# A decoder trunk on one core: the order in which two stages' weights are loaded and split

## The chip, the cores and the metric

The kernel runs on one core of a Trainium2 chip. The metric is the device time in microseconds (us) of one execution; the kernel before has a median of 1101.56 us over three runs (1101.03 to 1102.16).

## The reference

One layer of a decoder trunk on 512 positions of width 1024, in float32. Three token mixers work in parallel on a normalised input; their outputs are gated, projected and summed, the sum is projected once more, normalised and added to the input, and a SwiGLU block follows.

```python
gates = jax.nn.sigmoid(mg).reshape(B, S, N_BRANCH, D_MODEL)
merged = (gates[:, :, 0] * (y_a @ w_br_a)
          + gates[:, :, 1] * (y_b @ w_br_b)
          + gates[:, :, 2] * (y_c @ w_br_c))
x = x + rms_norm(merged @ w_o, g_post_mix)

hf = rms_norm(x, g_pre_ffn)
f_gate, f_up = jnp.split(hf @ w_ffn_in, 2, axis=-1)
f = (jax.nn.silu(f_gate) * f_up) @ w_ffn_out
return x + rms_norm(f, g_post_ffn)
```

The change lies between the gate and projection of the second branch (`y_b @ w_br_b`) and the first products with `w_ffn_in`.

## The kernel before, in words

**Split matmuls.** Every matrix is multiplied at float32 accuracy out of fast `fp32r` matmuls: a weight tile of 128x1024 is loaded as it is (`raw`), ScalarE copies it into a rounded `hi` (line 131), VectorE computes the rest `lo = raw - hi` (line 136), and TensorE adds three products, `hi*x_hi`, `hi*x_lo` and `lo*x_hi`. So each weight tile costs one DMA of 512 KB on SyncE's queue, one ScalarE and one VectorE instruction, and it must have passed all three before TensorE comes to it. The `raw` tiles have two buffers: the load of a tile waits for the `lo` of the tile two places earlier in that ring.

**The weight list.** `wlist` holds the tiles in the order of their use. `wload(upto)` issues load and split of all tiles below `upto`, but not beyond `wlimit`; `unit()` hands out the next tile and calls `wload` for two further ones. `tc.issue_after(ins)` keeps what is issued inside it behind the instruction `ins` in the engines' order; without it the layer that orders the program may put it earlier. Each engine then carries out its own list strictly in that order. `B0 + j` are the gate tiles 0 to 7 of branch b, `B0 + 8 + k` (k = 0 to 7) the tiles of `w_o`, and `W0 + i` (`W0 = B0 + 16`; i = 0 to 3) the first gate/up tiles of `w_ffn_in`. The text calls them gate j, w_o k and fi i.

**The stages around the change.**
- `b_stage` computes branch b's gates (`b_gate`, 24 matmuls of 128x512 each) and its projection in four pairs (`b_pair(0)` to `b_pair(3)`, 84 matmuls of 128x256 each). A pair's weights are loaded by `b_raw` into `raw` tiles (pairs 0 and 1) or into another slab (`rawb`), and are turned by `b_prep` into sums and splits (lines 1124 to 1163): `a22`, then the differences of lines 1141, 1142, 1152, 1153, and the splits that give `a11`, `s2`, `a12`, `s1`/`s4`, `s3`. Within a pair, ScalarE empties the one accumulator `z` between products (lines 1186 to 1205), and the next product on `z` waits for that copy. `i` in `b_stage` counts a pair's steps.
- `wo_pass(0)` and `wo_pass(2)` multiply by `w_o` (line 1332): each pass takes two of the four row chunks, goes through the eight tiles of `w_o` in order, and makes 12 matmuls with each. The tiles stay for the second pass. A pass uses four of six accumulator banks, so the second pass takes its third and fourth bank from the first pass, whose results must have been read by then.
- Beside `wo_pass(0)` run `row_loads` (rows of `x`, the gain vectors `gb`, and w_o tiles 4 to 7) and `first_weights`, which loads the first pair of gate/up tiles for the later stage (`rawp`, one DMA of 1 MB) and prepares it in `pair_prep` (lines 1548 to 1562: `s13`, `a22`, the sums of 1557 and 1559, and the splits). Here `s13` takes a `raw` buffer too.
- Beside `wo_pass(2)` run `wo_norm(0)` and `gain_late`. `wo_norm(0)` reads each bank of pass 0 twice: squares on ScalarE (line 1349, `junk`) and products with the gain on VectorE (line 1352, `yg`), which free the bank. `gain_late` scales the second gain vector.
- `ffn_head` multiplies by fi 0 to 3 (line 262), and `pairs` goes on with the rest.

**What sets the order.** The order on each engine comes from the order in which these generators issue, and from `issue_after`. In `b_stage` gate 4 is loaded by `b_more(1)` at step 3 of pair 0 and gate 5 by the `b_more(1)` behind that pair, which keeps it behind the pair's last copy of `z`; w_o 0 to 4 are issued at steps 1, 3, 5, 7 and 9 of pair 3, each behind the last copy of `z`; fi 0 and the next are issued by `unit()` towards the end of pass 0, since `wlimit` is already at its end.

Of the kernel before, what the change touches and what calls it, by code (L numbers as in the profile page):

```python
# [52 lines left out]
def hybrid_block(ctx: ExitStack, tc: tile.TileContext, A, out):  # L53
# [44 lines left out]
    def nm(s):  # L98
        cnt[0] += 1
        return f"{s}_{cnt[0]}"  # L100

    def slab(name, dt=F32, tag="slab", shape=(4, S), first=0):
        pool, bufs = (merge if tag == "m" else big, TAGS[tag]) if tag in TAGS else phase_pool[tag]
        if tag not in ("y", "mo", "f"):
            return pool.tile([128, *shape], dt, tag=tag, name=nm(name), bufs=bufs)
        size = 2064 if tag == "f" else 2112
        t = pool.tile([128, size], dt, tag=tag, name=nm(name), bufs=bufs)[:, first:first + math.prod(shape)]
        return t if len(shape) == 1 else t.rearrange(
            "p (a b) -> p a b" if len(shape) == 2 else "p (a b c) -> p a b c", **dict(zip("abc", shape)))

    def row(name, dt=F32, tag="row", first=0):
        bufs = {"row": 6, "q32": 2, "tg": 2}[tag]
        return mid.tile([128, S if tag == "row" else S + 32], dt, tag=tag, name=nm(name), bufs=bufs)[:, first:first + S]
# [13 lines left out]
    def f32(ap):  # L127
        return ap.bitcast(F32)

    def split(src, hi, lo, lo_eng=None):  # L130
        res["hi"] = SC.activation(hi, src, AF.Copy)  # L131
        e = lo_eng or V
        if e is GP:
            GP.tensor_sub(lo, src, f32(hi))
        else:
            res["lo"] = V.tensor_sub(lo, src, f32(hi))  # L136

    res = {}
# [32 lines left out]
    B0 = len(wlist)  # L171
# [5 lines left out]
    W0 = len(wlist) - 2 * HEAD  # L177
    WALL = len(wlist)
    wlimit = [B0 + 4]
# [13 lines left out]
    def wload(upto):  # L193
        while wnext[0] < min(upto, wlimit[0]):
            i = wnext[0]
            ap, tag = wlist[i]
            if isinstance(ap, tuple):
                hi = wts.tile([128, 1024], F32R, tag="hi", name=nm("hi"), bufs=3)
                lo = wts.tile([128, 1024], F32R, tag="lo", name=nm("lo"), bufs=3)
                fo["prep"](*ap, hi, lo)  # L200
                wready[i] = (hi, lo)
                wnext[0] += 1
                continue
            raw = stage.tile([128, 1024], F32, tag="raw", name=nm("raw"), bufs=2)
            parts = [slice(0, 512), slice(512, 1024)] if i == 0 else [slice(0, 1024)]
            for n, p in enumerate(parts):
                (SC if i == n == 0 else SY).dma_start(raw[:, p], ap[:, p])
                if i == 0:
                    x_in(n + 1)
            if i == W0:  # L210
                u = slab("u", F32R, tag, (2, 1024))
                near = row("uh", F32R, "tg", 32), row("ul", F32R, "q32", 32)
                split(raw[:, :512], *near)
                split(raw[:, 512:], u[:, 0, 512:], u[:, 1, 512:])
                wready[i] = tuple(Halved(near[n], u[:, n]) for n in range(2))
                wnext[0] += 1
                continue
            if tag == "gate":

                hi = lo = wts.tile([128, 1024], F32R, tag="hi", name=nm("hi"), bufs=3)  # L220
                SC.activation(hi, raw, AF.Copy)
                r, h = (t.rearrange("p (k m) -> p k m", m=128)[:, :, 64:] for t in (raw, hi))
                V.tensor_sub(h, r, f32(h))
                wready[i] = (hi, lo)
                wnext[0] += 1
                continue
            if tag:
                u = slab("u", F32R, tag, (2, 1024))
                hi, lo = u[:, 0], u[:, 1]
            else:  # L230
                hi = wts.tile([128, 1024], F32R, tag="hi", name=nm("hi"), bufs=3)
                lo = wts.tile([128, 1024], F32R, tag="lo", name=nm("lo"), bufs=3)
            todo = [(raw[:, p], hi[:, p], lo[:, p], V) for p in parts]
            if i == 0:
                wfirst.extend(todo)
            else:
                split(*todo[0])
            wready[i] = (hi, lo)
            wnext[0] += 1
# [41 lines left out]
    def x_in(k):  # L281
        SY.dma_start(xt[k], A["xT"][:, k, :])
# [830 lines left out]
    def b_raw(p):  # L1113

        if p < 2:
            br[p] = [stage.tile([128, 1024], F32, tag="raw", name=nm("raw"), bufs=2) for _ in range(2)]
        else:
            t = slab("rawb", tag="mo", shape=(2, 1024))
            br[p] = [t[:, i] for i in range(2)]
        for i in range(2):  # L1120
            SY.dma_start(br[p][i], A["w_br"][1, 2 * p + i])
# [3 lines left out]
    def b_prep(p):  # L1125

        r = br.pop(p)
        a11, a12, a21, a22 = (r[i // 2][:, i % 2 * 512:i % 2 * 512 + 512] for i in range(4))
        w = bw[p] = {}

        def pair_unit():
            return tuple(wts.tile([128, 1024], F32R, tag=t, name=nm(t), bufs=3) for t in ("hi", "lo"))

        def halves(u, *names):
            for i, n in enumerate(names):
                w[n] = tuple(t[:, 512 * i:512 * i + 512] for t in u)

        w["a22"] = row("a22h", F32R), row("a22l", F32R)
        split(a22, *w["a22"])
        with tc.issue_after(res["lo"].ins):  # L1140
            V.tensor_sub(a21, a11, a21)
        V.tensor_add(a22, a22, a21)
        yield
        halves(pair_unit(), "a11", "s2")
        split(a11, *w["a11"])
        split(a22, *w["s2"])
        yield
        tag = ("q32", "tg")[p % 2]
        w["a12"] = row("a12h", F32R, tag, 32), row("a12l", F32R, tag, 0)
        split(a12, *w["a12"])  # L1150
        yield
        V.tensor_sub(a11, a22, a11)
        V.tensor_sub(a12, a12, a22)
        yield
        u = pair_unit()
        split(r[0], *u)
        halves(u, "s1", "s4")
        yield
        halves(pair_unit(), "s3")
        split(a21, *w["s3"])  # L1160
        yield

    def b_gate(j):

        ps = bank("mm")
        yield from matrix(ps, hh, hl)
        if j == 2:
            mg["rows"] = slab("tanh", tag="gb")
        t = mg["b", j] = row("tg", tag="tg") if j < 2 else mg["rows"][:, j % 4]
        res["tanh"] = SC.activation(t, ps, AF.Tanh, scale=0.5)  # L1170
# [55 lines left out]
    def b_more(n):  # L1226

        wlimit[0] += n
        with tc.issue_after(res["out"].ins):
            wload(wlimit[0])  # L1230

    def b_stage():

        for p in (0, 2, 3):
            b_raw(p)
        prep = b_prep(0)

        def begin():
            yield from yb_split(2)
            rest = yb_rest()  # L1240
            for g in (prep, prep, rest, rest, prep, prep, prep, rest, rest, prep, rest):
                next(g)
                yield

        run([b_gate(2), b_gate(3)], begin(), 1.5)
        for p in range(4):
            pair = b_pair(p)
            gates = {0: (4, 5), 1: (6,), 2: (7,), 3: ()}[p]
            prep = b_prep(p + 1) if p < 3 else iter(())
            for i, _ in enumerate(pair, 1):  # L1250
                if p < 3:
                    if i == 3:
                        b_more(1)
                    if p and i in (4, 5, 6, 7, 9):
                        next(prep)
                else:
                    if i == 1:
                        wlimit[0] = WALL
                    if i == 2:
                        low_late()  # L1260
                    if i in (1, 3, 5, 7, 9):
                        with tc.issue_after(res["out"].ins):
                            wload(B0 + 9 + (1, 3, 5, 7, 9).index(i))
            if p == 0:
                b_more(1)
                b_raw(1)
                next(prep)
            for n, j in enumerate(gates):
                side = iter(()) if p else itertools.islice(prep, 3 if n == 0 else 1)
                run([b_gate(j)], side, 1.0)  # L1270
            for _ in prep:
                pass
# [36 lines left out]

    def gain_late():  # L1310

        for _ in range(4):
            yield 1
        V.tensor_scalar(res["gb"][:, 1], res["gb"][:, 1], -0.5, None, op0=OP.mult)

    def wo_pass(c0):

# [687 lines left out]
```

## Time and profile before

| | |
|---|---|
| median of three runs | 1101.56 us (1101.03 to 1102.16) |
| the profiled execution | 1103.44 us, of which its span is 1101.7 us |
| TensorE busy | 1090.3 us, 99% of the span |
| VectorE busy | 855.5 us, 78% |
| ScalarE busy | 642.7 us, 58% |
| granted TensorE clock, mean | 0.998 |

In a row of the timeline stand the start and the duration in us, the engine, the line, the operation, the tiles as out<-in, and the count; a bracket tells how long the engine stood idle before it and what it waited for. A DMA-issue row has the engine SPq. Matmuls overlap: a 128x512 matmul shows 0.39 us, though one starts every 0.227 us in a full stream.

### The profile page before, as it was taken

The numbers are of one execution on the slowest core, as the hardware profiler recorded it, in microseconds if no ns is written. First come the engines' busy times: TensorE is split into PE (matmuls) and PEld (weight loads), VectorE is DVE, ScalarE is ACT, GpSimd is POOL, SyncE is SP. The second block draws the span as 40 slices with busy tenths as digits, with TensorE's granted clock in tenths as the row PEclk, the third lists the DMA queues.
The fourth block names the chain that finished last, engine by engine and source line by source line (L and its number), as shares of the span: only waits on it lengthen the run. The fifth ranks groups of instructions, "written<-read, shape, count | busy, mean of one in ns | idle before, by whom it ended". The sixth has DMA issues, their size and how long they took to land.

```text
span 1101.7 us, 16368 instructions
## 1 busy us (share of the span) xinstructions
PE 1090.3 (99%) x6296; PEld 946.7 (86%) x6296; DVE 855.5 (78%) x1500; ACT 642.7 (58%) x1167; POOL 46.3 (4%) x59
## 2 busy tenths in 40 slices
PE   9999999999999999999999999999999999999997
PEld 8888778888888888898888788987999999998886
DVE  6966968263576799998998887867988888889665
ACT  6756674232344676877777655545666565667552
POOL 1000203010000000000000000000000000022200
PEclk9999999999999999999999999999999999999999
DMA  8322325322322210202111134172223233378902
GB/s 314 115 96 77 97 83 189 129 77 97 94 84 90 77 58 20 78 20 77 59 38 59 58 115 134 40 256 69 78 96 120 92 118 114 134 199 224 181 29 95
DMA packets 34941, 115.04 MB, mean 104 GB/s; under 512 B 3440, under 2 KB 3728, under 8 KB 33968
## 3 DMA queue, kind: packets, MB, share of 16 engines
q1 hardware_dynamic: 28064, 96.93, 25.8%
q0 software_dynamic: 5216, 11.18, 5.1%
q10 hardware_dynamic: 1584, 5.90, 1.4%
q8 instruction: 49, 0.80, 0.3%
q14 instruction: 28, 0.23, 0.1%
HBM read 111.89 MB, written 2.10 MB: 103 GB/s over the span
## 4 chain that ended last, share of the span: by engine, by line
PE 91%; DVE 4%; DMA 2%; ACT 2%; issue 1%; DVEq 0%; ACTq 0%
PE mm L262 37%; PE mm L1570 17%; PE mm L1706 7%; PE mm L565 4%; PE o L915 4%; PE sc L877 3%; PE mm L1182 3%; PE tr L902 3%; PE tr L1706 3%; PE mm L793 2%; PE mm L1332 2%; PE tr L709 1%; DMA raw<-in_w_o 1%; DVE lo L136 1%; PE mm L1434 1%; PE tr L490 1%
## 5 line engine op out<-in xcount | busy, mean ns | idle before, releaser
L262 PE MATMUL mm<-hh,hi 128*128 128x512 f32 x504 | 199.6, 396 | 0.0
L262 PE MATMUL mm<-hh,lo 128*128 128x512 f32 x504 | 197.6, 392 | 0.2 <-DVE lo L136 0.2
L262 PE MATMUL mm<-hl,hi 128*128 128x512 f32 x504 | 197.1, 391 | 0.0
L131 ACT ACTIVATE hi<-raw 128x1024 fp32r<-128x1024 f32 (+1 forms) x108 | 110.7, 1026 | 119.1 <-PE mm L262 55.6
L136 DVE TENSOR_TENSOR lo<-raw,hi 128x1024 fp32r<-128x1024 f32 (+1 forms) x108 | 128.3, 1189 | 63.1 <-ACT hi L131 56.8
L262 PEld LDWEIGHTS mm<-hh,lo 128*128 128x128 f32 x504 | 94.7, 188 | 19.9 <-DVE lo L136 0.5
L262 PEld LDWEIGHTS mm<-hh,hi 128*128 128x128 f32 x504 | 94.7, 188 | 18.5 <-ACT hi L131 0.4
L262 PEld LDWEIGHTS mm<-hl,hi 128*128 128x128 f32 x504 | 94.7, 188 | 18.4 <-issue 0.2
L883 ACT ACTIVATE P<-P,ast 128x128 f32<-128x128 f32 (+3 forms) x128 | 70.7, 555 | 23.4 <-DVE ast L881 22.7
L881 DVE CUSTOM_DVE_ANT_0 P<-sc,mask 128x128 f32<-128x128 f32 (+3 forms) x128 | 57.9, 484 | 8.1 <-PE sc L877 7.2
L131 ACT ACTIVATE ph<-tr 128x512 fp32r<-128x512 f32 x80 | 46.9, 592 | 26.0 <-PE tr L902 24.1
L136 DVE TENSOR_TENSOR pl<-tr,ph 128x512 fp32r<-128x512 f32 x80 | 54.4, 685 | 3.0 <-PE o L915 0.9
L1657 POOL DMA_DIRECT2D bs<-in_w_fo x16 | 19.3, 1213 | 781.0 <-DVE lo L136 781.0
L877 PE MATMUL sc<-K,q 128*128 128x512 f32 (+2 forms) x192 | 51.0, 368 | 0.2 <-DVE ast L881 0.2
L1570 PE MATMUL mm<-t,hi 128*128 128x256 f32 x288 | 50.9, 276 | 0.0
L1706 PE MATMUL mm<-hi,u 128*128 128x512 f32 x160 | 50.4, 390 | 0.1
L902 PE MATMUL tr<-ident,P 128*128 128x128 f32 x320 | 48.7, 273 | 0.0
L902 PEld LDWEIGHTS tr<-ident,P 128*128 128x128 f32 x320 | 39.0, 140 | 9.8 <-DVE pl L136 1.1
L136 DVE TENSOR_TENSOR lo<-bs,hi 128x1024 fp32r<-128x1024 f32 x28 | 34.1, 1221 | 13.6 <-ACT hi L131 13.5
L1570 PEld LDWEIGHTS mm<-t,hi 128*128 128x128 f32 x288 | 43.4, 188 | 0.0
L1570 PE MATMUL mm<-fh,hi 128*128 128x256 f32 x144 | 40.1, 278 | 0.0
L1570 PE MATMUL mm<-t,lo 128*128 128x256 f32 x144 | 39.8, 276 | 0.0
(451 smaller groups left out, 2838.1 us busy)
## 6 DMA issues: line engine op xcount, KB each, us to landing
raw<-in_w_in SPq DMA_DIRECT2D x64, 512.0 KB, 3.5
rawp<-in_w_fi SPq DMA_DIRECT2D x20, 1024.0 KB, 4.9
raw<-in_w_br SPq DMA_DIRECT2D x20, 512.0 KB, 3.5
bs<-in_w_fo POOLq DMA_DIRECT2D x20, 512.0 KB, 6.7
w<-in_cw ACTq DMA_DIRECT2D x4, 1024.0 KB, 5.8
raw<-in_w_o SPq DMA_DIRECT2D x8, 512.0 KB, 3.7
bs<-in_w_fo SPq DMA_DIRECT2D x8, 512.0 KB, 7.5
raw<-in_w_v SPq DMA_DIRECT2D x7, 512.0 KB, 5.0
```

Source lines behind the costliest of these rows:

```text
L131: res["hi"] = SC.activation(hi, src, AF.Copy)
L136: res["lo"] = V.tensor_sub(lo, src, f32(hi))
L262: res["mm"] = PE.matmul(ps[:m, n0:n1], w[:, k * 128:k * 128 + m], x[k][:, n0:n1], start=(t == 0), stop=(t == 3 * NK - 1))
L565: res["mm"] = PE.matmul(b[c], x[k][:, c * 128:(c + 1) * 128], w[:, kk * 512:kk * 512 + 512], start=(k == 0 and t == 0), stop=(k == NK - 1 ...
L877: PE.matmul(ps[:, :w * n].rearrange("p (b n) -> p b n", b=w), lhs, K[:, i, brs[0]:brs[-1] + 1, :n], start=(i == 0), stop=(i == 1))
L881: V.tensor_tensor_reduce(out=t, in0=ps[:, b * n:b * n + n], in1=mask[0][:, S - n:], scale=-0.125, scalar=3.0e38, op0=OP.add, op1=OP.min, a ...
L883: SC.activation(t, t, AF.Exp, scale=-1.0, bias=st[:, 0, j, b:b + 1], accum_out=st[:, 1, j, b:b + 1])
L902: PE.transpose(pt[:, j * 128:(j + 1) * 128], self.part(j, br)[:, kt * 128:(kt + 1) * 128], ident)
L915: PE.matmul(po, VV[:, kt, g % 2, br].rearrange("p i d -> p (i d)"), x, start=(br == 0 and kt == 0 and t == 0), stop=(br == 1 and kt == a a ...
L1182: res["mm"] = PE.matmul(ps, u[:, k * 128:k * 128 + 128], v[:, k], start=(start and k == t == 0), stop=(k == 3 and t == 2), skip_group_chec ...
L1570: res["mm"] = PE.matmul(ps, w[:, k * 128:k * 128 + 128], x[:, k], start=(start and k == t == 0), stop=(k == 3 and t == 2), skip_group_chec ...
L1706: PE.matmul(ps, a, b, start=id(ps) not in begun, stop=i == len(ops) - 1, skip_group_check=True)
```

## The change

Three edits.
- Gate 5: where `b_more` raises the limit to `B0 + 6`, its load and split are no longer kept behind the last copy of `z`.
- w_o 0 to 4 are issued at steps 1, 2, 3, 5 and 7 of pair 3 instead of 1, 3, 5, 7 and 9, the first two of them without `issue_after`.
- The limit in pair 3 is `W0` instead of the end, so that `unit()` no longer issues fi 0 in pass 0. `gain_late` raises it at its second step and issues fi 0, then fi 1 and fi 2 each two steps later; fi 3 comes by `unit()`.

```diff
--- before.py
+++ after.py
@@ -1226,7 +1226,7 @@
     def b_more(n):
 
         wlimit[0] += n
-        with tc.issue_after(res["out"].ins):
+        with tc.issue_after(res["out"].ins) if wlimit[0] != B0 + 6 else nullcontext():
             wload(wlimit[0])
 
     def b_stage():
@@ -1255,12 +1255,12 @@
                         next(prep)
                 else:
                     if i == 1:
-                        wlimit[0] = WALL
+                        wlimit[0] = W0
                     if i == 2:
                         low_late()
-                    if i in (1, 3, 5, 7, 9):
-                        with tc.issue_after(res["out"].ins):
-                            wload(B0 + 9 + (1, 3, 5, 7, 9).index(i))
+                    if i in (1, 2, 3, 5, 7):
+                        with tc.issue_after(res["out"].ins) if i > 2 else nullcontext():
+                            wload(B0 + 9 + (1, 2, 3, 5, 7).index(i))
             if p == 0:
                 b_more(1)
                 b_raw(1)
@@ -1309,9 +1309,16 @@
 
     def gain_late():
 
-        for _ in range(4):
+        for n in range(4):
             yield 1
+            if n == 1:
+                wlimit[0] = WALL
+                wload(W0 + 1)
         V.tensor_scalar(res["gb"][:, 1], res["gb"][:, 1], -0.5, None, op0=OP.mult)
+        for n in (2, 3):
+            yield 1
+            yield 1
+            wload(W0 + n)
 
     def wo_pass(c0):
```

No matmul, split or DMA is added or taken away. What moves on the engines, at the three places that the prediction speaks of:

ScalarE at the end of pair 0, before: `hi_6046` is gate 5's split, `hi_5981` gate 4's, `hi_6067` belongs to pair 1, `L1198` and `L1205` empty `z`.

```order
L131 ACTIVATE hi_5981<-raw_5979 128x1024
L1198 ACTIVATE r_1030_5936<-mm_5933 128x256
L131 ACTIVATE a12h_6232<-rawb_5831 128x512
L1205 ACTIVATE r_1030_5936<-mm_5933 128x256
L131 ACTIVATE hi_6046<-raw_6044 128x1024
```

And now:

```order
L131 ACTIVATE hi_5981<-raw_5979 128x1024
L131 ACTIVATE hi_6046<-raw_6044 128x1024
L1198 ACTIVATE r_1030_5936<-mm_5933 128x256
L131 ACTIVATE a12h_6232<-rawb_5831 128x512
L1205 ACTIVATE r_1030_5936<-mm_5933 128x256
```

Gate 5's copy has moved up past the two copies of `z`. On VectorE its `lo_6047` has moved in the same way, to right behind gate 4's `lo_5982`, ahead of lines 1199 to 1213; the load that waits for it on SyncE, the second half of pair 1's weights (`raw_6051`), keeps its place in the queue.

ScalarE from the end of pair 2 into pair 3, before (`u` are the w_o tiles; `mh` the merged rows, `L1186` to `L1198` empty pair 3's `z` and `y`):

```order
L1215 ACTIVATE mh_6412<-merged_1723 128x512 x2
L131 ACTIVATE hi_6449<-rawb_5834 128x512
L1170 ACTIVATE tanh_5878<-mm_6423 128x512
L1186 ACTIVATE r_1092_6455<-mm_6453 128x256
L131 ACTIVATE u_6475<-raw_6473 128x1024
L1190 ACTIVATE r_1093_6456<-mm_6454 128x256
L1193 ACTIVATE r_1092_6455<-mm_6453 128x256
L131 ACTIVATE u_6509<-raw_6507 128x1024
L1198 ACTIVATE r_1093_6456<-mm_6453 128x256
L131 ACTIVATE u_6540<-raw_6538 128x1024
```

And now (`u_6475`, `u_6496`, `u_6514`, `u_6545` are w_o 0 to 3):

```order
L1215 ACTIVATE mh_6412<-merged_1723 128x512
L131 ACTIVATE u_6475<-raw_6473 128x1024
L1215 ACTIVATE mh_6412<-merged_1723 128x512
L131 ACTIVATE u_6496<-raw_6494 128x1024
L131 ACTIVATE hi_6449<-rawb_5834 128x512
L1170 ACTIVATE tanh_5878<-mm_6423 128x512
L1186 ACTIVATE r_1092_6455<-mm_6453 128x256
L1190 ACTIVATE r_1093_6456<-mm_6454 128x256
L1193 ACTIVATE r_1092_6455<-mm_6453 128x256
L131 ACTIVATE u_6514<-raw_6512 128x1024
L1198 ACTIVATE r_1093_6456<-mm_6453 128x256
L131 ACTIVATE u_6545<-raw_6543 128x1024
```

w_o 0 and 1 have moved up from inside pair 3 to the end of pair 2, and w_o 2 and 3 by one copy of `z` each. On SyncE w_o 4's load now stands ahead of the two rows of `x`, and w_o 6's ahead of `rawp`.

VectorE at the end of pass 0, before: `u_6624` is w_o 6, `lo_6643` w_o 7, `s_1131`, `lo_6694`, `lo_6696`, `a22l` and the `rawp` rows belong to the first gate/up pair, `ul` is the first half of fi 0, `yg` frees a bank of pass 0.

```order
L136 TENSOR_TENSOR u_6624<-raw_6622,u_6624 128x1024
L1548 TENSOR_TENSOR s_1131_6701<-rawp_6609 128x1024
L136 TENSOR_TENSOR lo_6643<-raw_6640,hi_6642 128x1024
L136 TENSOR_TENSOR lo_6694<-rawp_6609,hi_6693 128x1024
L136 TENSOR_TENSOR lo_6696<-s_1131_6701,hi_6695 128x1024
L1557 TENSOR_TENSOR rawp_6609<-s_1131_6701,rawp_6609 128x512
L1352 TENSOR_TENSOR yg_6763<-mm_6594,gb_6584 128x512
L1314 TENSOR_SCALAR gb_6584<-gb_6584 128x1024
L136 TENSOR_TENSOR ul_6707<-raw_6703,uh_6706 128x512
L136 TENSOR_TENSOR a22l_6728<-rawp_6609,a22h_6727 128x512
L1352 TENSOR_TENSOR yg_6767<-mm_6595,gb_6584 128x512
```

And now:

```order
L136 TENSOR_TENSOR u_6624<-raw_6622,u_6624 128x1024
L1555 TENSOR_TENSOR s_1131_6701<-rawp_6609 128x1024
L136 TENSOR_TENSOR a22l_6719<-rawp_6609,a22h_6718 128x512
L1564 TENSOR_TENSOR rawp_6609<-s_1131_6701,rawp_6609 128x512
L1566 TENSOR_TENSOR rawp_6609<-rawp_6609 128x512
L136 TENSOR_TENSOR lo_6643<-raw_6640,hi_6642 128x1024
L136 TENSOR_TENSOR lo_6694<-rawp_6609,hi_6693 128x1024
L136 TENSOR_TENSOR lo_6696<-s_1131_6701,hi_6695 128x1024
L1317 TENSOR_SCALAR gb_6584<-gb_6584 128x1024
L136 TENSOR_TENSOR ul_6800<-raw_6796,uh_6799 128x512
L1359 TENSOR_TENSOR yg_6749<-mm_6594,gb_6584 128x512
L1359 TENSOR_TENSOR yg_6753<-mm_6595,gb_6584 128x512
```

(Lines behind the change have numbers 7 higher in these rows.) `a22l` and the two sums on `rawp`, which stood behind w_o 7's `lo` and between the `yg`, now stand ahead of it, as `s` did already; the `yg` stand together, and both come behind `ul`. On ScalarE, in the same way, `a22h` of `rawp` stands ahead of w_o 7's `hi`, and fi 0's `uh` ahead of all the `junk`; fi 1 to 3 are split later than before.

## The prediction

> **What bounds the kernel now.** The page comes first: what share of the span has TensorE.
>
> ```profile
> span 1101.7 us, 16368 instructions
> PE 1090.3 (99%) x6296; PEld 946.7 (86%) x6296; DVE 855.5 (78%) x1500; ACT 642.7 (58%) x1167; POOL 46.3 (4%) x59
> ```
>
> TensorE is busy in 99% of the span. The change takes no matmul away, so it can win only where TensorE waits, in the stages that it touches. The view of waits, TensorE alone, from 640 to 810 us (columns: total, times, longest):
>
> ```profile
> PE mm L1332 <- DVE yg L1352: 0.8, 1, 0.8
> PE mm L1182 <- DVE lo L136: 0.7, 1, 0.7
> PE mm L1332 <- DVE u L136: 0.7, 1, 0.7
> ```
>
> Three waits, 2.2 us, are all there is. The timeline of TensorE shows where they lie; in each pair the second row is late. The two rows at 741.76 and 744.48 are the first matmul with w_o 7 and the first of the second pass.
>
> ```profile
> 682.33 0.28 PE L1182 MATMUL mm<-ybl,hi 128*128 128x256 f32 x1
> 683.34 0.39 PE L1182 MATMUL mm<-ybh,lo 128*128 128x256 f32 x1 [0.73 <-DVE lo L136]
> ...
> 735.05 0.80 PE L1332 MATMUL mm<-u,mh 128*128 128x512 f32 x2
> 735.69 0.40 PE L1332 MATMUL mm<-u,ml 128*128 128x512 f32 x1
> ...
> 738.02 0.40 PE L1332 MATMUL mm<-u,mh 128*128 128x512 f32 x1
> 739.14 0.50 PE L1332 MATMUL mm<-u,mh 128*128 128x512 f32 x1 [0.72 <-DVE u L136]
> ...
> 741.76 0.39 PE L1332 MATMUL mm<-hi,mh 128*128 128x512 f32 x1
> ...
> 744.48 0.61 PE L1332 MATMUL mm<-u,mh 128*128 128x512 f32 x2
> ...
> 746.52 0.39 PE L1332 MATMUL mm<-u,mh 128*128 128x512 f32 x1
> 747.73 0.50 PE L1332 MATMUL mm<-u,mh 128*128 128x512 f32 x1 [0.82 <-DVE yg L1352]
> ```
>
> Between 741.76 and 744.48 lie 12 matmuls, so one takes 0.227 us from start to start, and one of half the width about 0.114. What a wait costs is its start-to-start time less that: 1.01 - 0.11 = 0.90 us at 683.34 (first difference matrix `s1` of pair 1); 0.64 - 2 x 0.227 = 0.19 at 735.05 (w_o 5); 1.12 - 0.23 = 0.89 at 739.14 (w_o 6); 1.21 - 0.23 = 0.98 at 747.73 (a bank of pass 0). Together 2.96 us, 0.27% of the median. About 0.2%, 2.2 us, is what a measurement of this kernel can tell from no change.
>
> **Part 1, gate 5.** How the wait at 683.34 comes about, on three engines:
>
> ```profile
> 672.01 1.22 DVE L136 TENSOR_TENSOR lo<-raw,hi 128x1024 fp32r<-128x1024 f32 x1
> ...
> 673.26 0.33 SPq L1121 DMA_DIRECT2D raw<-in_w_br  x1
> ...
> 676.85 0.63 ACT L131 ACTIVATE a22h<-raw 128x512 fp32r<-128x512 f32 x1 [1.03 <-DMA raw<-in_w_br]
> ```
>
> Gate 5's `lo` ends at 673.23 and frees its buffer; pair 1's second load goes out at 673.26 and lands at 676.83; from `a22h` on, differences and splits follow one another up to `s1`'s `lo`, for which TensorE waits until 683.34. With gate 5's copy ahead of line 1198 the chain starts when its own load has landed, and that copy then stands before 1198:
>
> ```profile
> 662.03 0.33 SPq L207 DMA_DIRECT2D raw<-in_w_in  x1
> ...
> raw<-in_w_in SPq DMA_DIRECT2D x1, 512.0 KB, 4.9
> ...
> 667.36 0.38 ACT L1198 ACTIVATE r<-mm 128x256 f32<-128x256 f32 x1 [1.49 <-PE mm L1182]
> ...
> 668.20 0.39 PE L1182 MATMUL mm<-t,a22h 128*128 128x256 f32 x2
> ```
>
> Landed at 666.93, copied by 668.0, `lo` by about 669.3: 3.9 us earlier than now. The second load moves as much, so what follows it has room for 3.9 us where 0.90 is needed; even the 1.2 us by which lines 1199 to 1213 move back on VectorE don't use it up. The wait goes. The price: line 1198 starts at about 667.92 (copies of 1024 follow each other by 0.97: the 1.06 less some overlap) and ends at 668.30 instead of 667.74, and the `a22` product waits for it: 0.16 us. Gain 0.90 - 0.16 = 0.74.
>
> **Part 2, w_o.** Everything from here to the second pass moves with TensorE, so I keep the clock of the trace before. Now the w_o tiles on ScalarE, and `lo` of w_o 5 and 6:
>
> ```profile
> 723.43 1.05 ACT L131 ACTIVATE u<-raw 128x1024 fp32r<-128x1024 f32 x1
> ...
> 727.17 1.06 ACT L131 ACTIVATE u<-raw 128x1024 fp32r<-128x1024 f32 x1 [1.65 <-DMA raw<-in_w_o]
> ...
> 732.98 1.06 ACT L131 ACTIVATE u<-raw 128x1024 fp32r<-128x1024 f32 x1 [4.75 <-DMA raw<-in_w_o]
> 736.76 1.06 ACT L131 ACTIVATE u<-raw 128x1024 fp32r<-128x1024 f32 x1 [2.72 <-DMA raw<-in_w_o]
> ...
> 734.07 1.23 DVE L136 TENSOR_TENSOR u<-raw,u 128x1024 fp32r<-128x1024 f32 x1 [3.11 <-ACT u L131]
> 737.86 1.23 DVE L136 TENSOR_TENSOR u<-raw,u 128x1024 fp32r<-128x1024 f32 x1 [2.56 <-ACT u L131]
> ```
>
> These are w_o 3, 4, 5, 6; the last three wait for their loads, each of which waits for a buffer that a `lo` two tiles back frees. With w_o 0 and 1 split at the end of pair 2 and 2 and 3 one copy of `z` earlier, each tile comes to the place of the one before it: w_o 4 is split at 723.43, 5 at 727.17, 6 at 732.98, 7 can be copied from 736.76. On SyncE the sequence of w_o 4, two rows of `x`, w_o 5, a gain, w_o 6, `rawp`, w_o 7 is then the old one with w_o counted up by one, at the same issue times. w_o 6's `lo` ends at 735.30 instead of 739.09; it is needed at 739.14 less the wait of 0.89 and the 0.19 before it, 738.06. w_o 5's ends by 729.5. Both waits go, 1.08 us, and the cover is 2.7 us.
>
> **Part 3, the second pass.** Freed of these, w_o 7 begins at 741.76 - 1.08 = 740.68, the second pass at 743.40, and its third bank is wanted six matmuls later, at 744.76. Here the new order of VectorE decides. `rawp`'s load and rows of the old order:
>
> ```profile
> L1529 SPq DMA_DIRECT2D rawp<-in_w_fi x1: 433/433/433, 726.1 to 726.1; - x1
> DMA to landing us min/median/max: 9.3/9.3/9.3
> ...
> 739.12 1.23 DVE L1548 TENSOR_TENSOR s<-rawp 128x1024 f32<-128x1024 f32 x1
> 740.26 1.22 DVE L136 TENSOR_TENSOR lo<-raw,hi 128x1024 fp32r<-128x1024 f32 x1
> ...
> 743.66 0.68 DVE L1557 TENSOR_TENSOR rawp<-s,rawp 128x512 f32<-128x512 f32 x1
> 744.27 0.68 DVE L1352 TENSOR_TENSOR yg<-mm,gb 128x512 f32<-128x512 f32 x1
> ...
> 741.51 0.33 SPq L207 DMA_DIRECT2D raw<-in_w_fi  x1
> raw<-in_w_fi SPq DMA_DIRECT2D x1, 512.0 KB, 3.6
> ...
> 745.11 0.63 ACT L131 ACTIVATE uh<-raw 128x512 fp32r<-128x512 f32 x1 [1.10 <-DMA raw<-in_w_fi]
> 745.78 0.69 DVE L136 TENSOR_TENSOR ul<-raw,uh 128x512 fp32r<-128x512 f32 x1 [0.23 <-ACT uh L131]
> ```
>
> `rawp` lands at 735.4. `s` then starts at 735.5; 1.14 later `a22l` (739.12 to 740.26), 0.61 later line 1557 (743.66 to 744.27), 0.72 later line 1559, which needs its predecessor's end, 0.61 later w_o 7's `lo`: 738.5 to 739.8, in time for 740.9. That frees the buffer for fi 0, which lands 3.6 us later at 743.4; `uh`, 0.67 later `ul`, 0.61 later the first `yg`, done after 0.68: 745.4. ScalarE's `junk`, behind `uh` too, is through before. So the third bank comes 0.66 us after 744.76; the fourth follows in time. The wait of 0.98 is not removed but becomes one of 0.66: gain 0.32. The splits of fi 1 to 3 move back by up to some microseconds, into a pass whose remaining 84 matmuls, 19 us, and `ffn_head`'s products with fi 0 cover them; without that cover a tile's load, copy and `lo`, 3.6 + 1.06 + 1.23, would count.
>
> **The sum.** 0.74 + 1.08 + 0.32 = 2.1 us. The profiled execution, 1103.44 us (span 1101.7 and 1.7 around it), would become 1101.3; it stands 1.9 us above the median of the runs, so the median goes from 1101.56 to 1099.4.
>
> What the trace of before does not show is how `rawp` and w_o 7 land with the second gain and the last row of `x` in flight behind them, since these now go out at about 730 instead of 735.7. Nearest rows, the gain and the row behind w_o 7 as they are now:
>
> ```profile
> gb<-in_grow SPq DMA_DIRECT2D x1, 512.0 KB, 5.4
> ...
> x<-in_x SPq DMA_DIRECT2D x1, 512.0 KB, 6.1
> ```
>
> Against fi 0, alone in 3.6, the gain lost 1.8 us and the row 2.5. `rawp` can hardly land earlier than it does now with the same loads ahead of it, but by up to these two delays, 4.3 us, later. I take no delay, by the row of `rawp` itself, which already has a load behind it. A rule of the Trainium skill speaks against that: by "DMA: Bandwidth & Descriptors", section "Queues, rings and completion order", a later transfer may finish its write before an earlier one, since data descriptors carry no barrier. By it the delay needn't be nought; at 1 us the sum is 1.1. The rows quoted here landed in the order of their issue.
>
> **The rivals.**
> - *All waits go.* If fi 0 lands 0.7 us sooner than worked out (some DMA share is free then), the third bank is in time: 0.74 + 1.08 + 0.98 = 2.8 us, 1098.8. For it: 0.66 is small beside landing times of 3.6 to 9.3. Against it: it hangs on five steps in a row, each with its row. Chance 0.2.
> - *The w_o loads don't land earlier*, because the rows of `x`, the gain and `rawp` fill the queue and the extra tile in it only waits longer: w_o 6's `lo` still ends at 739.1, `s` follows it, and the chain of part 3 starts 3.6 us later. Its end then comes at 0.66 + 3.6 = 4.2 us of lateness against 2.06 now: 2.2 lost, 0.74 won in part 1, 1103.0. Against it: issue times and what is ahead in the queue are those of a row that exists. Chance 0.1.
> - *Slower: `rawp` comes last.* Now w_o 7's `lo` stands behind three more operations on `rawp` and fi 0 behind that. Each microsecond that `rawp` lands later is one microsecond more at the third bank; from 2.1 us on nothing is won. If it shares the engines with the gain and the row issued behind w_o 7 and bears both their delays, 4.3 us, the bank comes 5.0 us late against 2.06 now: 2.9 lost, 0.74 won, 1103.8. For it: VectorE is strictly in that order. Against it: `rawp` goes out about 4 us ahead of the two. Chance 0.06.
> - The change does do what it says: the orders show it.
>
> **How the numbers follow.** The forecast has 0.6 of the chance, 0.04 is left for the unforeseen. Its own range, with `rawp` or fi 0 0.5 us early or 0.9 late, is 1098.9 to 1100.3, on both sides of the 0.2% line at 1099.36. The range for 8 in 10 reaches from all waits gone, less 0.2 for the runs' own spread, 1098.6, to `rawp` 1.6 us late, 1101.0. Faster: the second case and somewhat under half of the first, 0.46; slower: 0.06; the same: 0.48.
>
> **What would show it.** Right: no wait at pair 1's `s1` and at w_o 5 and 6; `a22` of pair 0 late by about 0.16; a wait of 0.3 to 1 us at the second pass's third bank, ended by `yg`, with fi 0's landing, `uh`, `ul` and `yg` in a row before it. Wrong: a wait at w_o 7 or a `rawp` landing over 10 us after its issue (third rival); w_o 6 still split after 736 (second); no wait at the bank (first).

## The result, and the profile after

The kernel after takes 1108.27 us in the median of six runs (1107.06 to 1110.01), before beside it 1101.70 (1101.03 to 1102.22): 1.0062 of before, with an interval of 1.0049 to 1.0075. So the change makes the kernel slower by some 6.6 us, where 1099.4 was forecast. The profiled execution of after took 1107.06 us; the two profiled executions stand on different sides of their medians (before 1.7 us above it, after 1.2 below), so their spans differ by 3.3 us only. The page of after:

```profile
span 1105.0 us, 16374 instructions
PE 1095.8 (99%) x6296; PEld 953.2 (86%) x6296; DVE 856.3 (77%) x1500; ACT 643.5 (58%) x1167; POOL 46.5 (4%) x59
```

TensorE is busy 5.5 us longer with the same 6296 instructions. In the view of waits TensorE's list from 640 to 815 us is empty: all the waits that the prediction priced are gone. The windows of TensorE show the same (columns: window, its length, busy time and matmuls, granted clock, DMA share, GB/s). First before, then after:

```profile
680.00:720.00 40.00, 39.27 (x291) 1.00 0.19 67
720.00:750.00 30.00, 28.46 (x131) 1.00 0.72 245
...
790.00:985.00 195.00, 194.90 (x1706) 1.00 0.34 114
```

```profile
680.00:720.00 40.00, 40.00 (x301) 1.00 0.25 85
720.00:750.00 30.00, 30.00 (x137) 1.00 0.63 222
...
790.00:985.00 195.00, 195.00 (x1658) 1.00 0.32 110
```

In the first two windows after does more matmuls. In the third both are busy throughout (before all but 0.1 us) at the full clock, and after does 48 fewer in the same time. To see what each stage won or lost in these two executions, take the first matmul of pair 0, of `wo_pass(0)`, of `ffn_head` and of the stage behind `pairs` from the timeline of TensorE. Before:

```profile
659.67 0.28 PE L1182 MATMUL mm<-ybh,hi 128*128 128x256 f32 x1
...
721.43 0.63 PE L1332 MATMUL mm<-u,mh 128*128 128x512 f32 x2
...
769.36 0.50 PE L262 MATMUL mm<-fh,u 128*128 128x256 f32 x2
...
983.55 0.39 PE L1706 MATMUL mm<-hi,u 128*128 128x512 f32 x1
```

After:

```profile
660.04 0.28 PE L1182 MATMUL mm<-ybh,hi 128*128 128x256 f32 x1
...
720.47 0.63 PE L1339 MATMUL mm<-u,mh 128*128 128x512 f32 x2
...
766.01 0.50 PE L262 MATMUL mm<-fh,u 128*128 128x256 f32 x2
...
986.98 0.40 PE L1713 MATMUL mm<-hi,u 128*128 128x512 f32 x1
```

| stage | before, us | after, us | difference |
|---|---|---|---|
| up to pair 0 | 659.67 | 660.04 | +0.37 |
| branch b's pairs | 61.76 | 60.43 | -1.33 |
| both passes of w_o | 47.93 | 45.54 | -2.39 |
| `ffn_head` and `pairs` | 214.19 | 220.97 | +6.78 |
| to the end of the span | 118.15 | 118.02 | -0.13 |

Between these two executions the change wins 3.7 us where it was meant to, and loses 6.8 us in the stage behind it, where TensorE waits for nothing. There the matmuls themselves are slower: more time passes from the start of one to the start of the next. That time is called the pace here, and a stall is a place where a matmul starts late because it had to wait. One place shows the pace best, the product of fi 0 with the second half of the positions (weight tiles `uh`, `ul`), in the timeline of TensorE of before:

```profile
784.79 0.28 PE L1570 MATMUL mm<-fl,hi 128*128 128x256 f32 x1
...
785.38 0.28 PE L1434 MATMUL mm<-fh,uh 128*128 128x256 f32 x1
...
786.74 0.28 PE L1434 MATMUL mm<-fh,u 128*128 128x256 f32 x1
```

Five matmuls lie between the first two of these rows, 0.118 us each; the product that begins at 785.38 has twelve, 0.113 each. After, at the same place:

```profile
781.46 0.28 PE L1577 MATMUL mm<-fl,hi 128*128 128x256 f32 x1
...
782.05 0.28 PE L1441 MATMUL mm<-fh,uh 128*128 128x256 f32 x1
...
783.46 0.28 PE L1441 MATMUL mm<-fh,u 128*128 128x256 f32 x1
```

Nothing changes here: 0.118 ahead of 782.05 and 1.41 / 12 = 0.1175 behind it. And so it stays to the end of `pairs`, in windows of 100 us, of before and of after:

```profile
880.00:980.00 100.00, 100.00 (x885) 1.00 0.36 126
```

```profile
880.00:980.00 100.00, 100.00 (x851) 1.00 0.33 118
```

About two matmuls more than are started reach into a window, so 100 / 883 = 113.2 ns in the one and 100 / 849 = 117.8 ns in the other. There are two paces, 4.5 ns or 4% apart, and nothing between: before changes to the fast one at 785.38, falls back at 814.05 and at 862 and is fast again some 10 us later each time; after has 1746 matmuls in the slow pace from 781.25 to 986.86. The 1573 that are fast in before make 7.1 us at 4.5 ns, of which the 6.8 are what before's own stalls leave.

### The profile page after: what moved, and what is told of

The parts are those of the page before. It is cut to its first block, busy times and chain, and to the rows that moved or that the text cites. A ratio compares the mean times of both kernels' runs of the same rounds, so it can differ in the third digit from the quotient of the medians.

```text
span 1105.0 us, 16374 instructions
## 1 busy us (share of the span) xinstructions
PE 1095.8 (99%) x6296; PEld 953.2 (86%) x6296; DVE 856.3 (77%) x1500; ACT 643.5 (58%) x1167; POOL 46.5 (4%) x59
## 4 chain that ended last, share of the span: by engine, by line
PE 94%; DVE 3%; ACT 1%; DMA 1%; issue 0%; SPq 0%; DVEq 0%; ACTq 0%
PE mm L262 38%; PE mm L1577 18%; PE mm L1713 6%; PE mm L1339 4%; PE o L915 4%; PE mm L565 3%; PE mm L1182 3%; PE sc L877 3%; PE tr L902 3%; PE tr L1713 3%; PE mm L793 2%; PE tr L709 1%; PE mm L1441 1%; PE tr L490 1%; DVE lo L136 1%; PE tr L625 1%
## 5 line engine op out<-in xcount | busy, mean ns | idle before, releaser
L1664 POOL DMA_DIRECT2D bs<-in_w_fo x16 | 19.3, 1213 | 783.9 <-DVE lo L136 783.9
L1577 PE MATMUL mm<-fl,hi 128*128 128x256 f32 x144 | 40.2, 279 | 0.0
```

Source lines behind the costliest of these rows:

```text
L1577: res["mm"] = PE.matmul(ps, w[:, k * 128:k * 128 + 128], x[:, k], start=(start and k == t == 0), stop=(k == 3 and t == 2), skip_group_chec ...
```

## The experiments

**What differs at these places.** The buffers of the tags `tg` and `q32` are handed out by turns, two of each, 544 elements or 2176 bytes apart, which is eight and a half times 256. Their users here are `uh` and `ul` (line 212, offset 32 elements) and each pair's `a22h` and `a22l`:

```python
        side = 32 * ((j - HEAD) % 2)
        w["a22"] = row("a22h", F32R, "tg", side), row("a22l", F32R, "q32", side)
```

32 elements are 128 bytes, so with the right turn every one of these tiles begins at the same place modulo 256. Before gives `uh` its buffer first, after gives it to the first pair's `a22` first, since fi 0 is now issued later. The numbers in the names of the rows quoted in the section on the change say so: `ul_6707` stands below `a22l_6728` before, and `a22l_6719` below `ul_6800` after. With that, every turn from there on is swapped against `side`. In the two built programs `uh` and the `a22h` begin at bytes 30080 and 32128 by turns before, 128 modulo 256, and at 29952 and 32256 after, 0 modulo 256. All other weights of the stage stand at 0 in both, and all its moving operands at 64.

**Placement theory.** The pace is a state, which lasts once it is set. A product whose weights stand at 128 modulo 256 behind others at 0 switches TensorE to 113 ns, a stall drops it to 118 ns, and otherwise it stays. In after there is no such product left from fi 0 on.

**Timing theory.** Without its waits TensorE meets the other engines' and the DMA's accesses at other moments, and these slow its matmuls down. Then the pace goes with the order of the instructions and not with addresses.

The kernel before had medians of 1101.7 to 1103.1 us in the different groups of runs, so ratios to the before of the same group are compared.

**Placement and order apart.** `after_moved` is after, `before_moved` is before, both with this edit, which moves the tiles by 128 bytes; instructions and order stay.

```diff
-                near = row("uh", F32R, "tg", 32), row("ul", F32R, "q32", 32)
+                near = row("uh", F32R, "tg", 0), row("ul", F32R, "q32", 0)
...
-        side = 32 * ((j - HEAD) % 2)
+        side = 32 * ((j - HEAD + 1) % 2)
```

> The kernel after, with the four small weight tiles of gate/up that stand in the `tg` and `q32` buffers (a22 of each pair, and the first half of fi 0) put 128 bytes elsewhere in their buffers, so that they begin at 128 modulo 256 bytes as they did in the kernel before; the instructions and their order stay those of after. Placement theory (the 128x256 matmuls have two paces, 118 and 113 ns from start to start; a product with weights at 128 modulo 256 switches to 113, a stall switches back to 118): 113 ns from fi 0's second half of the columns on, at about 782 us, so some 1700 matmuls x 4.5 ns = 7.6 us less than after, of which up to 1 us is lost again to stalls: 1100.0 us (1099.0 to 1101.5). Timing theory (TensorE goes slower because, without its waits, it meets other engines' accesses at other moments): as after, 1108.3 us (1107.0 to 1110.0).

> The kernel before, with the same edit, which puts the same tiles at 0 modulo 256 bytes, as they stand in after; the instructions and their order stay those of before, with all its waits. Placement theory: 118 ns from 785 us to the end of the stage instead of 113 ns; before has 254 + 334 + 985 = 1573 matmuls there in the fast pace, x 4.5 ns = 7.1 us more: 1108.8 us (1107.5 to 1110.0). Timing theory: the order is before's, so 1101.7 us (1101.0 to 1102.3).

Measured: `after_moved` 1101.10 us beside 1103.12 of before, 0.9979 (0.9971 to 0.9988); `before_moved` 1109.39 us, 1.0056 (1.0043 to 1.0069). The same windows, of `after_moved`, then of `before_moved`:

```profile
786.00:798.00 12.00, 12.00 (x108) 1.00 0.01 3
...
880.00:980.00 100.00, 100.00 (x885) 1.00 0.39 130
```

```profile
786.00:798.00 12.00, 12.00 (x104) 1.00 0.01 2
...
880.00:980.00 100.00, 100.00 (x851) 1.00 0.34 117
```

885 and 851 matmuls, as in before and after, but with the orders exchanged. In the first window the DMA engines are nearly still in both, so it isn't their traffic either. The pace goes with the 128 bytes; the timing theory falls.

**The change's parts.** `gate5_and_wo` is after without the edits that delay fi 0, `gain_late_only` is before with them alone.

`gate5_and_wo` against after:

```diff
-                        wlimit[0] = W0
+                        wlimit[0] = WALL
...
-            if n == 1:
-                wlimit[0] = WALL
-                wload(W0 + 1)
...
-        for n in (2, 3):
-            yield 1
-            yield 1
-            wload(W0 + n)
```

> The change's first two edits alone (gate 5, and w_o 0 to 4 earlier); fi 0 is issued in pass 0, as before. Placement theory: fi 0 is given its buffers ahead of a22 as before, so the pace from 785 us on is before's; the waits at s1 and at w_o 5 and 6 go (0.90 + 1.08 = 1.98 us), and the 72 matmuls of pair 1 behind s1 run at 113 instead of 118 ns, 0.3 us more: 1099.4 us (1098.8 to 1100.3). Timing theory: it is the waits' going that slows the matmuls, so near after, 1106 to 1109 us.

> The change's third edit alone (fi 0 to 2 issued in gain_late); gate 5 and w_o as before. Placement theory: fi 0 is given its buffers behind a22, so the tiles stand at 0 modulo 256 and the stage runs at 118 ns, 7.1 us more, with the bank wait of 0.98 us perhaps shorter: 1108.5 us (1107.3 to 1109.8), although the waits at s1 and w_o are still there. Timing theory: the waits at s1 and w_o stay, and so does most of the pace: 1101.5 us (1100.7 to 1103.0).

Measured: `gate5_and_wo` 1101.20 us, 0.9981 (0.9972 to 0.9990); `gain_late_only` 1108.85 us, 1.0049 (1.0036 to 1.0062). The first lies above its expected range in us because before does too in this group; by the ratio it wins 0.19% where 0.21% was expected. The waits of TensorE from 640 to 1000 us, of `gate5_and_wo` (the banks of the second pass), of `gain_late_only` and of `before_moved` (both gate 5's):

```profile
PE mm L1332 <- DVE yg L1352: 1.3, 2, 1.0
...
PE mm L1182 <- DVE lo L136: 0.7, 1, 0.7
...
PE mm L1182 <- DVE lo L136: 0.6, 1, 0.6
```

So the first edit takes gate 5's wait away, and the third brings the loss, in an order that still has that wait. What the second and third edits win is less clear, since the waits at w_o 5, w_o 6 and the bank come and go with the execution. `before_moved` has before's order and none of them in its view, and both of its passes of w_o take 45.95 us, against 47.93 in before and 45.54 in after:

```profile
721.61 0.63 PE L1332 MATMUL mm<-u,mh 128*128 128x512 f32 x2
...
767.56 0.50 PE L262 MATMUL mm<-fh,u 128*128 128x256 f32 x2
```

A wait at the bank stands in four of the twelve profiles, two with fi 0 loaded as in before (`before` and `gate5_and_wo`) and two as in after (`quarter_offset`, 0.5 us, and `tokens_and_yb_moved`, 1.1 us, both introduced below). In these four `rawp` landed 9.2 to 9.9 us after its issue, in the other eight 7.2 to 8.2. That `after_moved` is no faster than `gate5_and_wo` (1101.10 and 1101.20) says that the third edit's own gain is too small to be seen.

**Is it a state?** `one_product` is after with the first pair's `a22` alone at 128 modulo 256, 12 matmuls.

```diff
-        side = 32 * ((j - HEAD) % 2)
+        side = 32 * (j == HEAD or (j - HEAD) % 2)
```

> The kernel after with a22 of the first pair alone put at 128 modulo 256 bytes: one product of 12 matmuls, at about 802 us; all other weights stay at 0 modulo 256. If the pace is a state that such a product switches and that lasts until a stall (placement theory): 113 ns from about 802 us on, though the later matmuls' own tiles are just those of after, and 118 ns again from the first stall to the end of the stage, since no product is left to switch it back. With a stall at the second pair's a22, as the moved kernel of after has one at 821 us, the gain is small, (821 - 802) / 0.113 x 4.5 ns = 0.8 us against after; with none it is 6.8 us: 1101.5 to 1109 us, and the trace says which. If each matmul's pace comes from its own addresses: 12 x 4.5 ns = 0.05 us, 118 ns all through the stage but for those 12, and the time of after.

Its timeline and windows of TensorE:

```profile
801.41 0.87 PE L1577 MATMUL mm<-t,u 128*128 128x256 f32 x6
802.11 0.39 PE L1577 MATMUL mm<-t,a22h 128*128 128x256 f32 x2
...
802.45 0.39 PE L1577 MATMUL mm<-t,a22h 128*128 128x256 f32 x2
```

```profile
786.00:801.00 15.00, 15.00 (x130) 1.00 0.01 2
802.00:858.00 56.00, 56.00 (x497) 1.00 0.34 114
862.00:980.00 118.00, 118.00 (x1043) 1.00 0.37 125
```

The first six take 0.70 us, 0.117 each; then three take 0.34. From there on the pace is 113 ns for the 178 us that are left, though every later tile stands where after has it. Twelve matmuls set the pace of some 1560. The times, 1103.30 us, 1.0007 (0.9994 to 1.0020), are in two groups: five of twelve from 1099.99 to 1100.75, one at 1102.57, six from 1104.03 to 1105.99. One execution only has a profile, so that the slower ones stalled is argued, not seen; the next pair makes the stall on purpose.

**What a stall costs.** In the seventh pair of the loop ScalarE copies `z` five times instead of once, so that the next `a22` has to wait; in `after_moved` and in `one_product`.

```diff
-            SC.activation(r2[:, 256:], z, AF.Copy)
+            for _ in range(5 if j == HEAD + 6 else 1):
+                SC.activation(r2[:, 256:], z, AF.Copy)
```

> after_moved with the copy of `z` behind s3 made five times instead of once in the seventh pair of the loop, so that its a22, at about 860 us, has to wait: the copy ended 354 ns ahead of that product in after_moved, and four more at 0.26 us from start to start end 0.7 us behind it. Placement theory: a stall of 0.7 us, then 118 ns for 84 matmuls, until the next pair's a22 at 128 modulo 256 switches back: 0.7 + 84 x 4.5 ns = 1.1 us more than after_moved, 0.9989 of before (0.9978 to 1.0002). If a stall costs its length alone: 0.7 us.

> one_product with the same five copies. Placement theory: 113 ns from 802 us to the stall at 860 us, then 118 ns to the end of the stage at 983 us in every execution, since no product there stands at 128 modulo 256 any more: 0.7 + (983 - 860) / 0.1133 x 4.5 ns = 0.7 + 4.9 = 5.6 us more than the 1100.2 us of one_product's undisturbed executions, 1105.8 us (1104.8 to 1107.5), without its executions at 1100 us. If a stall costs its length alone: 0.7 us more than one_product, 1101 to 1106.7 us by turns.

Measured: `moved_and_stall` 1102.88 us, 1.0000 (0.9990 to 1.0010), some 0.2% more than `after_moved`; `one_product_and_stall` 1106.92 us, 1.0038 (1.0023 to 1.0053), with no run under 1106.64. The stall and the windows around it in `moved_and_stall`:

```profile
858.99 0.28 PE L1577 MATMUL mm<-t,lo 128*128 128x256 f32 x1
860.61 1.09 PE L1577 MATMUL mm<-t,u 128*128 128x256 f32 x7 [1.35 <-ACT r L1605]
861.85 0.50 PE L1577 MATMUL mm<-t,a22h 128*128 128x256 f32 x2
862.19 0.29 PE L1577 MATMUL mm<-t,a22l 128*128 128x256 f32 x1
```

```profile
802.00:858.00 56.00, 55.91 (x490) 1.00 0.31 114
862.00:980.00 118.00, 118.00 (x1035) 1.00 0.35 120
```

And in `one_product_and_stall`:

```profile
859.49 0.28 PE L1577 MATMUL mm<-t,lo 128*128 128x256 f32 x1
860.68 1.09 PE L1577 MATMUL mm<-t,u 128*128 128x256 f32 x7 [0.91 <-ACT r L1605]
```

```profile
802.00:858.00 56.00, 56.00 (x496) 1.00 0.34 114
862.00:980.00 118.00, 118.00 (x1002) 1.00 0.33 112
```

A longer stall in the one (1.6 us from start to start) hardly changes the pace behind it, a shorter one in the other (1.2 us) leaves 1002 matmuls where `one_product` had 1043: 41 x 0.113 = 4.6 us lost behind the stall, besides the stall. The whole stop in `moved_and_stall`, ten matmuls from 858.99 to 862.19, takes 3.20 us instead of 1.13, and these 2.1 us are about all that it lost against `after_moved` (0.2%). The state, its fall by a stall and its return by a tile at 128 modulo 256 are shown. That `moved_and_stall` was back in the fast pace by 862.3, not 84 matmuls later as expected, I can't explain in full. Its `a22` at 128 modulo 256 came only seven matmuls behind the stall, at 861.85, and so could switch at once; but at 814.05 in before such a tile, held up at its start in the same way, was followed by the slow pace for 84 matmuls.

**Which addresses?** Three kernels, all after with one offset changed, ask what the rule is: `tokens_moved` moves the moving operands by 128 bytes, `tokens_and_yb_moved` also those of branch b, `quarter_offset` puts `a22` at 64 and 192 modulo 256.

```diff
-        fh, fl = res["fh"], res["fl"] = Pair("fh", F32R, "y", MOVED), Pair("fl", F32R, "y", MOVED)
+        fh, fl = res["fh"], res["fl"] = Pair("fh", F32R, "y", 48), Pair("fl", F32R, "y", 48)
...
-        t = {n: slab("t", F32R, "mo", (2, 4, 256), MOVED) for n in (1, 2, 3, 4)}
+        t = {n: slab("t", F32R, "mo", (2, 4, 256), 48) for n in (1, 2, 3, 4)}
```

`tokens_and_yb_moved` has these and

```diff
-            yb["h"], yb["l"] = Pair("ybh", F32R, "y", MOVED), Pair("ybl", F32R, "y", MOVED)
+            yb["h"], yb["l"] = Pair("ybh", F32R, "y", 48), Pair("ybl", F32R, "y", 48)
```

and `quarter_offset` has

```diff
-        side = 32 * ((j - HEAD) % 2)
+        side = 16
```

> The kernel after with the moving operands of the gate/up stage (`fh`, `fl`, and the four `t` of its token sums) 128 bytes further on in their buffers (offset 48 instead of 16 elements): all weights stay where after has them, at 0 modulo 256, but the moving operand minus the weights is now 192 modulo 256 in every product of the stage, as it was with a22 alone in before. If the difference of the two addresses sets the pace: every product switches to 113 ns, from the first at 766 us on, and a stall costs only its own length and a matmul or two: some 1850 matmuls x 4.5 ns = 8.3 us less than after, 1.0 us less than after_moved, so 0.9970 of before (0.9955 to 0.9980). If it is the weights' address alone: 118 ns all through, as after, 1.006 of before.

> tokens_moved with `ybh` and `ybl` moved by the same 128 bytes, so that branch b's four pairs switch to 113 ns with their first product instead of their second, and pair 0 recovers sooner from its stall at 663 us. Difference theory: 3 x 11 + some 60 matmuls x 4.5 ns = 0.4 us less than tokens_moved: 0.9966 of before (0.9950 to 0.9978). Weights' address alone: as after, 1.006 of before.

> The kernel after with a22 at offset 16 in both buffers: its weights begin at 64 and 192 modulo 256 bytes by turns, the moving operand minus the weights at 0 and 128. If only a difference of 192 switches the pace: 118 ns all through, as after (1.005 to 1.007 of before). If any difference other than 64 does: 113 ns from the first or the second pair's a22 on, at 802 or 812 us, 6 to 7 us less: 0.998 to 1.000 of before.

Measured: `tokens_moved` 1104.62 us, 1.0016 (1.0004 to 1.0029); `tokens_and_yb_moved` 1103.39 us, 1.0017 (1.0003 to 1.0031); `quarter_offset` 1107.42 us, 1.0050 (1.0037 to 1.0063). The first two fit neither reading. `tokens_moved`, with one difference of addresses all through:

```profile
786.00:910.00 124.00, 124.00 (x1090) 1.00 0.30 103
918.00:980.00 62.00, 62.00 (x529) 1.00 0.40 135
```

124 / 1088 = 114.0 ns, then, behind a short stall at 916.6, 62 / 527 = 117.6 ns to the end: both paces last at the same difference. And `quarter_offset`, whose total looks like after's:

```profile
790.00:803.00 13.00, 13.00 (x113) 1.00 0.01 2
805.00:812.00 7.00, 7.00 (x65) 1.00 0.42 146
815.00:860.00 45.00, 45.00 (x384) 1.00 0.28 94
```

By the same reckoning 117, 111 and 118 ns (the middle window is short, and its figure rough): the first pair's `a22`, at 64 modulo 256, did switch to the fast pace, and the second's, at 192, switched back. The time alone would have told the opposite. In branch b of `tokens_and_yb_moved`, where all these weights begin at 0 modulo 256, the pace even goes to and fro with the moving operand, without a stall: `t` begins at 64 there, `ybh` and `ybl` now at 192.

```profile
684.08 0.40 PE L1182 MATMUL mm<-t,hi 128*128 128x256 f32 x2
...
685.50 0.28 PE L1182 MATMUL mm<-ybh,hi 128*128 128x256 f32 x1
...
686.86 0.40 PE L1182 MATMUL mm<-t,hi 128*128 128x256 f32 x2
```

Twelve matmuls take 1.42 us with `t` and 1.36 with `ybh` and `ybl`. So neither the difference of the two addresses nor the weights' alone is the rule. In the gate/up stage what lasts is the state; what can switch it is a change of the relation or a stall.

## Why the prediction was wrong

- **The step that failed** is the sentence "The change takes no matmul away, so it can win only where TensorE waits, in the stages that it touches." It took the time of a matmul as given. The sum lacked a term of +6.8 us in `ffn_head` and `pairs`, a stage whose order the change hardly touches, and no rival had it: all three were about waits. The third rival was the slower one, with a chance of 0.06, but by a wait that did not come. The range ended 7 us short.
- **What could have been seen.** The order rows on record show the buffers' names change places, and the trace of before has both paces: 0.118 ahead of 785.38 and 0.113 behind it in the rows above. The division that I made, 12 matmuls of 512 into "one of half the width about 0.114", gave the fast pace and hid the other.
- **Part 1** was forecast at 0.74 and gave 1.33. The wait of 0.90 went, and with it a start-to-start of 0.23 behind it where 0.11 is usual; the 0.16 at pair 0's `a22` was not paid, since gate 5's copy began at 666.69 us, 0.6 earlier than worked out (by the clock of after); and the stall had cost pair 1 the fast pace too, for the 66 matmuls left of it: 66 x 4.5 ns = 0.30.
- **Parts 2 and 3** were forecast at 1.08 and 0.32 and gave 2.39 together: all three waits are gone in the profile of after (0.19, 0.89 and 0.98), and behind the two longer ones one start-to-start of 0.34 us instead of 0.227 had stood that the sum left out, another 0.2. At the bank it came out as the rival *all waits go* had it. The load of `rawp`, `s` behind it on VectorE, and `yg`, in after:

```profile
725.19 0.43 SPq L1536 DMA_DIRECT2D rawp<-in_w_fi  x1
```

```profile
733.15 1.23 DVE L1555 TENSOR_TENSOR s<-rawp 128x1024 f32<-128x1024 f32 x1 [0.51 <-DMA rawp<-in_w_fi]
...
742.14 1.88 DVE L1359 TENSOR_TENSOR yg<-mm,gb 128x512 f32<-128x512 f32 x3
```

  `rawp` landed 7.9 us after its issue, not 9.3, and with the other steps as worked out the first bank was free by 742.8, ahead of its use at 743.6. With 9.2 us, in `quarter_offset`, a wait of 0.5 stands at the bank, near the 0.66 that was worked out for 9.3: the chain of part 3 was right, and what it took as fixed, the landing, is not. The delay of up to 4.3 us that the third rival feared did not come: the longest landing in any profile is 9.9 us. The rule of the Trainium skill that the prediction quotes ("DMA: Bandwidth & Descriptors", section "Queues, rings and completion order") would have allowed one.
- The three terms made 2.1 us where the stages won 3.7, and in the runs `after_moved`, the same order without the loss, wins 0.21% (0.12 to 0.29), 1.3 to 3.2 us. That this meets the 2.1 is partly luck: parts 2 and 3 were priced from one execution, 1.7 us above its median, and `before_moved` shows the same order without these waits. In the slow pace no gain of the order is seen at all (1.0062 in after, 1.0056 in `before_moved`, intervals overlapping), and why is open. What was left out was three times as large as what was worked out.

## What to carry to other kernels

When a change alters the order in which rotating buffers are handed out, look at which tile now sits in which buffer, above all where the code has odd offsets: the same instructions on other addresses are another kernel. "99% busy" is no bound that can't move: divide a stretch by its matmuls, stage by stage, and ask why one stage has two answers. And a stall can cost more than its length: look at the pace of what follows it. Before a wait is priced, look whether it stands in a second execution too.

Of the versions tried, `after_moved` and `gate5_and_wo` beat both kernels, by 0.2% over before; the second needs no care for the turns, since it leaves fi 0 where it was.

## What the runs showed of the hardware

- Streams of 128x256 matmuls in `fp32r` with a new weight tile for each matmul run at 113.2 or 117.8 ns from start to start, at the same granted clock, and keep their pace for up to 1746 matmuls. A third, 120 ns, stands in before from 350 to 361 us, where moving operand and weights both begin at 0 modulo 256.
- A tile of weights at 128 modulo 256 among others at 0, with the moving operand at 64, switched to the fast pace 8 of the 10 times that it was met in the slow one without a stall in before. In the fast pace, a delay of 0.22 us at an `a22` (814 us) and one of some 0.02 us at another (862 us) were followed by the slow one there. What the chip does there is open. The Trainium skill, "TensorE: Matmul & The Clock Gate", section "Step-by-step: what each phase is for", says that streaming and weight loading have a read port each and that loading the next weights takes no read bandwidth from the running matmul. Here a shift of weights by 128 bytes changes the pace by 4%, so in these runs the pace is not independent of where the operands begin. Whether the ports are the reason is not shown.
